# Rotary embedding on one core: the last add writes fp32 into the tile of x, and the copy from bf16 to fp32 on ScalarE goes

## The chip, the cores and the metric

The kernel runs on one core of a Trainium2 chip. The metric is the device time of one execution in microseconds (us). All runs quoted here were with a granted clock of 1.00, unless the text says otherwise. In the profile's lines DVE is VectorE, ACT is ScalarE, POOL is GpSimd and SP is SyncE. A name such as L94 is line 94 of the kernel's file. "Load" is a transfer from HBM to the on-chip memory, "store" one back. Both use the same 16 DMA engines.

A profiled span is about 1.8 us shorter than the time of the same run. Where the text compares moments, it uses the span.

## The reference, cut to what matters

```python
def setup_inputs():
    batch, seq_len, num_heads, head_dim = (8, 2048, 16, 64)
    # x: (8, 2048, 16, 64) fp32; cos, sin: (2048, 32) fp32

def reference(x, cos, sin):
    x_pairs = x.reshape(batch, seq_len, num_heads, head_dim // 2, 2)
    x1, x2 = x_pairs[..., 0], x_pairs[..., 1]
    out1 = x1 * cos - x2 * sin
    out2 = x1 * sin + x2 * cos
    return np.stack([out1, out2], axis=-1).reshape(batch, seq_len, num_heads, head_dim)
```

Input and output are 67.1 MB each, and each byte is moved once. Little is computed for each byte.

## The kernel before

The work is cut into 16 tiles of 128 partitions x 8 rows x 1024 values (4.19 MB), which are kept in five buffers (NX = 5). A tile is worked on in two pieces of four rows (128x4096). The first and the last tile are cut finer, into 4 pieces each, so there are 36 pieces: 30 of 128x4096, 2 of 128x2048 and 4 of 128x1024. Each piece passes through these steps:

```python
    def halve(j):                      # ScalarE: fp32 -> bf16
        i, k0, k1 = pieces[j]
        halved[j] = hpool.tile([P, 4, HD], bf16, name="xh", bufs=3)
        nc.scalar.copy(out=halved[j][:, : k1 - k0], in_=tiles[i][:, k0:k1])

    def rotate(j):                     # VectorE: three bf16 operations
        # ... (views of the tables and of the piece)
        nc.vector.tensor_tensor(out=rows(qt), in0=rows(xh), in1=tab(s_tab), op=mult)
        nc.vector.tensor_tensor(out=rows(xh), in0=rows(xh), in1=tab(c_tab), op=mult)
        # q_swap reads qt with the two members of each pair exchanged
        nc.vector.tensor_tensor(out=xh3, in0=xh3, in1=q_swap, op=add)
        rotated[j] = xh

    def widen(j):                      # ScalarE: bf16 -> fp32, then the store from ScalarE's queue
        i, k0, k1 = pieces[j]
        nc.scalar.copy(out=tiles[i][:, k0:k1], in_=rotated.pop(j)[:, : k1 - k0])
        # ... for each run of rows that is complete:
        nc.scalar.dma_start(out=out_t[b, g, :, r0:r1], in_=tiles[i][:, r0:r1])
        if k1 == K and i + NX < n:
            load(i + NX)               # SyncE's queue; waits until the store has freed the buffer

    # ... loads of tile 0, cos, sin, tiles 1 to 4; tables s_tab and c_tab made in bf16
        halve(0)
        for j in range(len(pieces)):
            if j + 1 < len(pieces):
                halve(j + 1)
            rotate(j)
            widen(j)
```

## Time and profile before

| | before |
|---|---|
| time, median of 4 runs | 318.59 us (318.53 to 318.70) |
| profiled span | 316.9 us |
| VectorE busy | 223.2 us (70%) |
| ScalarE busy | 230.0 us (73%) |
| moved | 134.76 MB, 425 GB/s over the span |

The first lines are from the page of the kernel before. They give the busy time of each engine, the span in 40 equal slices (one digit is the busy share of a slice in tenths, 9 meaning 90% or more), then the share of the 16 DMA engines' span that each queue's packets took.

```profile
DVE 223.2 (70%) x111; ACT 230.0 (73%) x73; POOL 0.2 (0%) x4
...
DVE  0189999999999596693967939588440999999112
ACT  4078899999998692976949679495803999997322
...
DMA  7999999999999999999999999999999999999997
...
q1 hardware_dynamic: 3712, 67.63, 50.1%
q10 hardware_dynamic: 2736, 67.11, 49.1%
```

The DMA row is 9 in every slice but the first and the last, while both compute engines have slices well below 9, many of 3 to 7. And the two queues together take 50.1% + 49.1% = 99.2% of all 16 DMA engines' time. There is hardly any time in which a DMA engine does nothing.

The groups by shape (count, busy us, mean ns of one, idle time of the engine before them and what ended it) give the cost of each step of a piece:

```profile
L75 ACT CAST xh<-xt 128x4096 bf16<-128x4096 f32 x30 | 108.1, 3603 | 50.7 <-DMA xt<-in_x_dram 45.4 <-ACT xt L105 5.4
L105 ACT CAST xt<-xh 128x4096 f32<-128x4096 bf16 x30 | 108.1, 3602 | 2.1 <-DVE xh L100 1.8
L94 DVE TENSOR_TENSOR qt<-xh,s_tab 128x4096 bf16<-128x4096 bf16 x30 | 68.8, 2292 | 56.6 <-ACT xh L75 55.8
L100 DVE TENSOR_TENSOR xh<-xh,qt 128x4096 bf16<-128x4096 bf16 x30 | 68.8, 2292 | 1.0
```

The view of waits (total us, times, longest) says why the compute engines idle. VectorE waits for ScalarE, and ScalarE waits for loads:

```profile
DVE qt L94 <- ACT xh L75: 70.3, 26, 12.9
ACT xh L75 <- DMA xt<-in_x_dram: 61.6, 13, 12.7
```

The chain that ended last is mostly DMA:

```profile
DMA 62%; ACT 26%; DVE 4%; issue 3%; another core or an unknown queue 2%; SPq 1%; ACTq 1%
```

The trace's records of issue and landing show the rate. Stores 0 to 10 land at 59.7, 79.1, 98.4, 118.6 us and so on, on average 19.44 us apart, although the first stores are issued every 14.7 us (35.94, 50.66, 65.35, 80.03). In the steady part a tile takes the DMA about 19.36 us (8.39 MB in and out, 433 GB/s).

### The profile page before, as it was taken

The page shows a single profiled execution, that of the slowest core. Times are in us where ns is not written, and L with a number is a line of the kernel's source. Part 1 is how long each engine was busy: PE and PEld are TensorE (multiplying, and loading weights), DVE is VectorE, ACT ScalarE, POOL GpSimd, SP SyncE. Part 2 cuts the span into 40 slices and gives each one's busy share as a digit, 9 for nine tenths or more (in the row PEclk, how much of TensorE's full clock was granted, in tenths as well). Part 3 has the DMA queues.
Part 4 walks back from the last instruction along what each step waited for, and adds up shares of the span by engine and source line. Part 5 has one row for each costly group of instructions (what it writes and reads, how often), then busy time and mean ns, then how long its engine had stood idle before and what let it go on. Part 6 is the DMA issues. An engine that isn't in the chain of part 4 may idle for free.

```text
span 316.9 us, 352 instructions
## 1 busy us (share of the span) xinstructions
DVE 223.2 (70%) x111; ACT 230.0 (73%) x73; POOL 0.2 (0%) x4
## 2 busy tenths in 40 slices
DVE  0189999999999596693967939588440999999112
ACT  4078899999998692976949679495803999997322
POOL 0000000000000000000000000000000000000000
DMA  7999999999999999999999999999999999999997
GB/s 304 424 463 405 455 397 401 459 438 422 455 405 463 397 460 401 459 414 448 443 418 455 405 459 405 455 405 459 418 443 447 414 428 430 424 433 439 442 414 302
DMA packets 6451, 134.76 MB, mean 425 GB/s; under 512 B 689, under 2 KB 1201, under 8 KB 1969
## 3 DMA queue, kind: packets, MB, share of 16 engines
q1 hardware_dynamic: 3712, 67.63, 50.1%
q10 hardware_dynamic: 2736, 67.11, 49.1%
q14 instruction: 3, 0.02, 0.0%
HBM read 67.63 MB, written 67.11 MB: 425 GB/s over the span
## 4 chain that ended last, share of the span: by engine, by line
DMA 62%; ACT 26%; DVE 4%; issue 3%; another core or an unknown queue 2%; SPq 1%; ACTq 1%
DMA xt<-in_x_dram 31%; DMA out_dram<-xt 28%; ACT xt L105 14%; ACT xh L75 12%; DMA sin_sb<-in_sin_dram 4%; DVE xh L100 1%; DVE xh L95 1%; DVE qt L94 1%; SPq L70 1%; ACTq L109 1%; DVE s_tab L121 0%; SPq L115 0%; DVE s_tab L122 0%; ACTq L105 0%
## 5 line engine op out<-in xcount | busy, mean ns | idle before, releaser
L75 ACT CAST xh<-xt 128x4096 bf16<-128x4096 f32 (+2 forms) x36 | 116.1, 3224 | 66.9 <-DMA xt<-in_x_dram 61.6
L105 ACT CAST xt<-xh 128x4096 f32<-128x4096 bf16 (+2 forms) x36 | 116.0, 3223 | 14.8 <-DVE xh L100 14.4
L94 DVE TENSOR_TENSOR qt<-xh,s_tab 128x4096 bf16<-128x4096 bf16 (+2 forms) x36 | 74.0, 2055 | 71.2 <-ACT xh L75 70.3
L100 DVE TENSOR_TENSOR xh<-xh,qt 128x4096 bf16<-128x4096 bf16 (+2 forms) x36 | 74.0, 2055 | 1.2
L95 DVE TENSOR_TENSOR xh<-xh,c_tab 128x4096 bf16<-128x4096 bf16 (+2 forms) x36 | 74.0, 2055 | 1.2
L121 DVE CAST s_tab<-sin_sb 128x512 bf16<-128x512 f32 x1 | 0.5, 453 | 14.4 <-DMA sin_sb<-in_sin_dram 14.4
L75 ACT ACT_TABLE_LOAD x1 | 1.3, 1283 | 0.7 <-PEq L147 0.7
L123 DVE CAST c_tab<-cos_sb 128x1024 bf16<-128x1024 f32 x1 | 0.7, 684 | 0.0
L122 DVE TENSOR_SCALAR s_tab<-sin_sb 128x512 bf16<-128x512 f32 x1 | 0.4, 442 | 0.0
L147 POOL MEMSET const-bfloat16-1.0<- 128x1 bf16 x1 | 0.1, 101 | 0.0
L147 POOL MEMSET const-uint8-127<- 128x1 uint8 x1 | 0.1, 101 | 0.0
L147 POOL MEMSET const-float32-0.0<- 128x1 f32 x1 | 0.1, 98 | 0.2 <-issue 0.2
L147 POOL MEMSET const-float32-1.0<- 128x1 f32 x1 | 0.1, 98 | 0.0
## 6 DMA issues: line engine op xcount, KB each, us to landing
out_dram<-xt ACTq DMA_DIRECT2D x15, 4096.0 KB, 38.6
xt<-in_x_dram SPq DMA_DIRECT2D x14, 4096.0 KB, 26.6
xt<-in_x_dram SPq DMA_DIRECT2D x2, 2048.0 KB, 16.3
xt<-in_x_dram SPq DMA_DIRECT2D x4, 512.0 KB, 24.1
xt<-in_x_dram SPq DMA_DIRECT2D x2, 1024.0 KB, 19.9
out_dram<-xt ACTq DMA_DIRECT2D x1, 2048.0 KB, 17.6
out_dram<-xt ACTq DMA_DIRECT2D x1, 1024.0 KB, 11.7
out_dram<-xt ACTq DMA_DIRECT2D x2, 512.0 KB, 4.1
```

Source lines behind the costliest of these rows:

```text
L70: nc.sync.dma_start(out=tiles[i][:, k0:k1], in_=x_t[b, g, :, k0:k1])
L75: nc.scalar.copy(out=halved[j][:, : k1 - k0], in_=tiles[i][:, k0:k1])
L94: nc.vector.tensor_tensor(out=rows(qt), in0=rows(xh), in1=tab(s_tab), op=mult)
L95: nc.vector.tensor_tensor(out=rows(xh), in0=rows(xh), in1=tab(c_tab), op=mult)
L100: nc.vector.tensor_tensor(out=xh3, in0=xh3, in1=q_swap, op=add)
L105: nc.scalar.copy(out=tiles[i][:, k0:k1], in_=rotated.pop(j)[:, : k1 - k0])
L109: nc.scalar.dma_start(out=out_t[b, g, :, r0:r1], in_=tiles[i][:, r0:r1])
L121: nc.vector.tensor_copy(out=s2[:, :, 0], in_=sin_flat)
L122: nc.vector.tensor_scalar_mul(s2[:, :, 1], sin_flat, -1.0)
L123: nc.vector.tensor_copy(out=c_tab.rearrange("p g k (i j) -> p (g k i) j", j=2), in_=cos_sb.rearrange("p g c -> p (g c)").to_broadcast([P, ...
L147: nc = _bacc.Bacc("TRN2", target_bir_lowering=False, num_devices=1)
```

## The change

The intent is to relieve ScalarE. VectorE's add writes its fp32 result directly over x in its tile, so that the second ScalarE copy (116.0 us busy in all) is not needed.

```diff
-        nc.vector.tensor_tensor(out=xh3, in0=xh3, in1=q_swap, op=add)
-        rotated[j] = xh
 
-    def widen(j):
+        y3 = tiles[i][:, k0:k1].rearrange("p k (a j) -> p (k a) j", j=2)
+        nc.vector.tensor_tensor(out=y3, in0=xh3, in1=q_swap, op=add)
+
+    def finish_piece(j):
         i, k0, k1 = pieces[j]
-        nc.scalar.copy(out=tiles[i][:, k0:k1], in_=rotated.pop(j)[:, : k1 - k0])
         g, b = groups[i]
 ...
             rotate(j)
-            widen(j)
+            finish_piece(j)
```

More of the change, by code (lines that the diff above doesn't have):

```diff
@@ L63 @@
         pieces += [(i, k0, k1) for k0, k1 in runs]
-    tiles, halved, rotated = {}, {}, {}
+    tiles, halved = {}, {}
     def load(i):
```

## The prediction

> **What bounds the kernel now.** The page's first two parts say DMA: the DMA row is 9 in all of the 40 slices but the first and last, at 425 GB/s over the 316.9 us span, while VectorE is busy 223.2 us (70%) and ScalarE 230.0 us (73%). The chain that ended last is 62% DMA. In the trace's issue and landing records, stores 0 to 10 land 19.3 to 20.2 us apart although ScalarE could prepare a tile every 14.7 us (stores issued at 35.94, 50.66, 65.35, 80.03); each load is issued when a store has freed its buffer. So a tile (4.19 MB in, 4.19 MB out) costs 19.36 us of DMA, 433 GB/s, and compute waits for it: the wait view has ScalarE waiting 61.6 us for loads and VectorE 70.3 us for ScalarE.
>
> **What the change does.** It removes 36 ScalarE copies (116.0 us busy), mostly off the bounding resource. It adds no instruction, but VectorE's final add now writes fp32. Today all three 4096-element VectorE operations take 2.292 us. The Trainium skill, "VectorE: DVE Perf Modes", section "The perf-mode tier table", gives a two-tensor operation double rate in bf16 only; its errata section gives (N+151)/0.96 ns for the fp32 add. The trace agrees with the same fixed term at double rate: (2048+151)/0.96 = 2291. So I expect the add at 4.42 us for 4096 elements, 2.29 for 2048, 1.22 for 1024. Bytes moved do not change.
>
> **The sum.** A full piece on VectorE goes from about 6.98 to 9.12 us with gaps, a tile from 14.0 to 18.24 us. All pieces: 30 x 9.12 + 2 x 4.84 + 4 x 2.71 = 294 us. VectorE busy becomes about 292 us (92%), ScalarE 114 us. VectorE starts rotating at 15.71 us as now (after the sin load), so unstarved it ends at about 310 us.
>
> **What is on the critical path.** 18.24 us per tile is below DMA's 19.36 by only 1.1 us. Store 0 is issued at about 35.1 us, and store i at about 35.1 + 18.24 i, always before store i-1 lands (about 39.5 + 19.36 i). So the store queue never runs dry, loads land almost when they do now, and each before VectorE needs it: tile 6 at about 105 us against 123, tile 14 at 260 against 269. VectorE runs nearly without a break, its backlog shrinking until the last pieces. The last row's load lands at about 308 us as now; VectorE is done with everything before at about 307. Then: halve 1.05, three operations 2.7, store 3.6. The removed last widening (1.04 us) is offset by 0.53 us of slower add. I expect under 1 us of change: the removed ScalarE work was hidden under DMA.
>
> **Predicted:** 318.0 us, 8 in 10 within 316.0 to 320.5. Faster by over 2%: 0.02; within 2%: 0.91; slower by over 2%: 0.07.
>
> **What the profile would show.** Add 4424 ns in the groups by form; VectorE 92%, ScalarE 36%; DMA row still 9s, about 426 GB/s; VectorE's waits for ScalarE fall from 70 us to under 10.
>
> **What would make it wrong.** Slack at the end is only 1 to 2 us, so an add above 4.5 us, or VectorE waiting for ScalarE (whose queue also holds the stores: store 11 now waits until 242.1 us for a load that shares its semaphore), would make it VectorE-bound at 320 to 325 us. If the mixed-type add kept double rate, DMA would still set the time, about 317.5 us.

## The result, and the profile after

| | before | after |
|---|---|---|
| time, median of 4 runs each | 318.59 us | 318.88 us (318.65 to 318.89) |
| ratio, 95% interval | | 1.0007 (0.9990 to 1.0024): the same |
| VectorE busy | 223.2 us (70%) | 291.4 us (92%) |
| ScalarE busy | 230.0 us (73%) | 116.3 us (37%) |
| one add of 128x4096 | 2.292 us | 4.425 us |

Ratios here and below are the mean time of one kernel's fast runs over that of the other's fast runs of the same rounds, so not quite the ratio of the medians quoted.

The same lines of the page, for the changed kernel:

```profile
DVE 291.4 (92%) x111; ACT 116.3 (37%) x37; POOL 0.2 (0%) x4
...
DVE  0199999999999999999999999999999999999993
ACT  4244441707044170805326080532608044350220
...
DMA  8999999999999999999999999999999999999997
...
q1 hardware_dynamic: 3712, 67.63, 50.1%
q10 hardware_dynamic: 2736, 67.11, 49.1%
```

ScalarE's busy time has halved and VectorE's row is now 9 in all slices but the first two and the last. The DMA row (but for its first slice) and the 99.2% have not moved, and neither has the time.

The groups by shape show the cost of the add, and the waits show that VectorE no longer waits for ScalarE at all. The roles have turned round: ScalarE waits 181.6 us for VectorE.

```profile
L102 DVE TENSOR_TENSOR xt<-xh,qt 128x4096 f32<-128x4096 bf16 x30 | 132.7, 4425 | 1.0
L75 ACT CAST xh<-xt 128x4096 bf16<-128x4096 f32 x30 | 107.1, 3604 | 164.5 <-DVE xt L102 159.2 <-DMA xt<-in_x_dram 5.2
L94 DVE TENSOR_TENSOR qt<-xh,s_tab 128x4096 bf16<-128x4096 bf16 x30 | 68.8, 2292 | 3.1
...
L102 DVE TENSOR_TENSOR xt<-xh,qt 128x1024 f32<-128x1024 bf16 x4 | 4.9, 1224 | 0.1
L102 DVE TENSOR_TENSOR xt<-xh,qt 128x2048 f32<-128x2048 bf16 x2 | 4.6, 2291 | 0.1
```

```profile
ACT xh L75 <- DVE xt L102: 181.6, 18, 11.3
DVE s_tab L121 <- DMA sin_sb<-in_sin_dram: 15.0, 1, 15.0
ACT xh L75 <- DMA xt<-in_x_dram: 9.7, 6, 2.8
```

The chain that ended last is now VectorE:

```profile
DVE 92%; DMA 4%; issue 2%; SPq 1%; DVEq 0%
```

This is a trap for a reader of profiles. The chain names VectorE for 92% of the span, yet the DMA engines are as full as they were. Two resources are at their limit at once, and a chain can follow only one of them. Which of them sets the time cannot be read from this page. The experiments decide it.

The timeline (start, duration, engine, line, operation) of one piece of the changed kernel gives VectorE's pitch: from 100.17 to 109.35 us is 9.18 us for a piece, so 18.36 us for a tile, against 19.36 us for the DMA.

```profile
100.17 2.29 DVE L94 TENSOR_TENSOR qt<-xh,s_tab 128x4096 bf16<-128x4096 bf16 x1
102.50 2.29 DVE L95 TENSOR_TENSOR xh<-xh,c_tab 128x4096 bf16<-128x4096 bf16 x1
104.82 4.43 DVE L102 TENSOR_TENSOR xt<-xh,qt 128x4096 f32<-128x4096 bf16 x1
109.28 0.34 ACTq L109 DMA_DIRECT2D out_dram<-xt  x1
109.35 2.29 DVE L94 TENSOR_TENSOR qt<-xh,s_tab 128x4096 bf16<-128x4096 bf16 x1
```

### The profile page after: what moved, and what is told of

It is laid out like the page before. It is cut to its first block, busy times and chain, and to the rows that moved or that the text cites. A ratio compares the mean times of both kernels' runs of the same rounds, so it can differ in the third digit from the quotient of the medians.

```text
span 317.1 us, 345 instructions
## 1 busy us (share of the span) xinstructions
DVE 291.4 (92%) x111; ACT 116.3 (37%) x37; POOL 0.2 (0%) x4
## 4 chain that ended last, share of the span: by engine, by line
DVE 92%; DMA 4%; issue 2%; SPq 1%; DVEq 0%
DVE xt L102 45%; DVE qt L94 23%; DVE xh L95 23%; DMA sin_sb<-in_sin_dram 4%; SPq L70 1%; DVEq L94 0%; DVE s_tab L121 0%; SPq L115 0%; DVE s_tab L122 0%; DVE c_tab L123 0%
## 5 line engine op out<-in xcount | busy, mean ns | idle before, releaser
L75 ACT CAST xh<-xt 128x4096 bf16<-128x4096 f32 (+2 forms) x36 | 115.1, 3224 | 191.4 <-DVE xt L102 181.6
L102 DVE TENSOR_TENSOR xt<-xh,qt 128x4096 f32<-128x4096 bf16 (+2 forms) x36 | 142.2, 3951 | 1.2
```

The lines of the kernel that those rows point to most:

```text
L102: nc.vector.tensor_tensor(out=y3, in0=xh3, in1=q_swap, op=add)
```

## The experiments

The theory T is that the transfers set the time of both kernels, and that VectorE's slower add just fits beside them. The rival R1 is that the change had two real effects that cancel, a gain from ScalarE and a loss from the add. The rival R2 is that VectorE alone sets the time of the changed kernel, as its chain says. Twelve kernels were run. "Wrong result on purpose" means that the arithmetic was cut for the sake of the measurement.

| run | result | median us | kernel before, same chip | ratio (95% interval) |
|---|---|---|---|---|
| dma_only | wrong | 318.16 | 318.80 | 0.9989 (0.9972 to 1.0005) |
| short_widen | wrong | 323.58 | 318.80 | 1.0132 (1.0096 to 1.0169) |
| half_widen | wrong | 318.90 | 318.67 | 1.0007 (0.9992 to 1.0022) |
| fp32_add_keep_copy | right | 324.65 | 318.80 | 1.0177 (1.0163 to 1.0190) |
| mixed | right | 318.73 | 318.80 | 0.9998 (0.9986 to 1.0010) |
| before_plus | right | 318.84 | 318.60 | 1.0006 (0.9993 to 1.0019) |
| after_plus | right | 318.79 | 318.60 | 1.0003 (0.9991 to 1.0015) |
| mixed_plus | right | 318.76 | 318.60 | 1.0005 (0.9993 to 1.0017) |
| after_plus_wide | right | 332.67 | 318.67 | 1.0434 (1.0416 to 1.0452) |
| after_tables_first | right | 320.60 | 318.60 | 1.0062 (1.0037 to 1.0087) |
| before_half_loads | wrong | 265.19 | 318.68 | 0.8321 (0.8308 to 0.8333) |
| after_half_loads | wrong | 317.22 | 318.68 | 0.9953 (0.9937 to 0.9970) |

### The transfers alone

```diff
-        halve(0)
         for j in range(len(pieces)):
-            if j + 1 < len(pieces):
-                halve(j + 1)
-            rotate(j)
             finish_piece(j)
```

> All loads and stores stay, all halving, rotating and widening goes (wrong result on purpose). Theory T (the 134.76 MB at about 433 GB/s set the time of both kernels): 316 to 318.5 us, at most 0.7% under the kernel before. Rival R1 (the change had two real effects that cancel: less ScalarE work gains, a slower add loses): the time falls well below both, under 310 us, since both are gone. Rival R2 (the changed kernel is set by VectorE alone and the transfers have room): also under 310 us.

Measured: 318.16 us. From its page:

```profile
DVE 1.4 (0%) x3; POOL 0.2 (0%) x4
...
DMA  8999999999999999999999999999999999999997
```

With no work on the pieces at all, the kernel takes what both kernels take, to within 0.3%. T holds and R1's gain has no room to exist: with these transfers in these queues, less than 1 us can be won from the kernel before by removing compute.

### VectorE alone, and ScalarE alone: half of the loads taken away

```diff
-        for k0, k1 in load_runs(i):
+        for k0, k1 in (load_runs(i) if i in (0, n - 1) else [(0, 4)]):
...
-        nc.scalar.copy(out=halved[j][:, : k1 - k0], in_=tiles[i][:, k0:k1])
+        r0 = k0 if i in (0, n - 1) else 0
+        nc.scalar.copy(out=halved[j][:, : k1 - k0], in_=tiles[i][:, r0 : r0 + k1 - k0])
```

The same edit was made to both kernels.

> The kernel before, but of tiles 1 to 14 only rows 0 to 3 are loaded and both pieces are halved from them (wrong result on purpose): 29.4 MB less to load, compute as it was. T: the transfers no longer set the time; ScalarE does, at 14.7 us a tile: about 258 to 268 us, faster by 16 to 19%.

> The changed kernel with the same 29.4 MB less to load. Its VectorE work has no gaps today, so T says that it takes over as the limit at once: 317 to 319 us, at most 0.6% faster, with the DMA row well below 9. If the transfers alone had set the time, it would fall as the kernel before does.

Measured: 265.19 us and 317.22 us. First the page of the kernel before with half loads (engines' busy time, ScalarE's row, DMA's row):

```profile
DVE 223.2 (85%) x111; ACT 230.1 (87%) x73; POOL 0.2 (0%) x4
...
ACT  4029799999999999999999999999999999999760
...
DMA  7999959797999999999999999999999999996997
```

Then the page of the changed kernel with half loads (engines' busy time, VectorE's row, DMA's row):

```profile
DVE 291.4 (92%) x111; ACT 115.9 (37%) x37; POOL 0.2 (0%) x4
...
DVE  0199999999999999999999999999999999999995
...
DMA  7999678978787895978879697877969966290996
```

Relieved of 29.4 MB, the kernel before falls to the next limit, ScalarE, which is then at 9 from the sixth slice to the fourth from the end, and issues a store every 14.66 us. Its DMA row is still 9 nearly everywhere (a tile's 6.29 MB at 433 GB/s would take 14.5 us, by calculation), so here too two limits lie close together, and compute by itself may need a little less than 265 us. The changed kernel falls by 0.5% only, with a DMA row that has slices of 5 and 6 and even 0: VectorE's work by itself takes 317.2 us. So the changed kernel has two limits within 1 us of each other, 318.2 us for the transfers and 317.2 us for VectorE. Before the change the compute engines had at least 53 us of room under the DMA limit (318.7 - 265.2); the change has used nearly all of it.

### Each half of the change alone

The first half: the bf16 add stays, and the ScalarE copy is cut to 16, then to 512, of every 1024 columns.

```diff
-        nc.scalar.copy(out=tiles[i][:, k0:k1], in_=rotated.pop(j)[:, : k1 - k0])
+        nc.scalar.copy(
+            out=tiles[i][:, k0:k1, :16], in_=rotated.pop(j)[:, : k1 - k0, :16]
+        )
```

> The kernel before with its bf16 add, but the ScalarE copy writes only 16 of every 1024 columns (wrong result on purpose), so the ScalarE work goes alone, without the slower add. T: 317 to 319 us, no gain above 0.5%, ScalarE busy falls to about 125 us. R1: faster by over 1%, since the gain is no longer paid back by the add.

> The kernel before with a ScalarE copy of 512 of every 1024 columns (wrong result on purpose): half of the ScalarE work that the change removes, with the bf16 add. T: removing it gains nothing: 317.5 to 319.5 us. If less ScalarE work itself makes the transfers slower, as the run with 16 columns could be read, about 320 to 322 us, with load packets that take longer than 1213 ns in each tile. R1: about half of a gain, under 316 us.

Measured: 323.58 us with 16 columns (six runs, 321.12 to 324.84) and 318.90 us with 512. In neither case is there a gain, so R1's gain is not seen. With 512 columns T's range holds. With 16 columns T's range was missed on the other side: less ScalarE work made the kernel 1.3% slower. The trace's packet records tell how, though not why. A packet of 32 KB takes 1213 ns on its DMA engine nearly always, and 16 engines x 32768 bytes / 1213 ns = 432 GB/s is the rate that all these kernels reach. In the run with 16 columns 370 such packets took over 1230 ns, in the kernel before 39, and in the run with 512 columns 43. The excess over 1213 ns, summed over the packets and divided by 16, is 3.8 us against 0.8 and 0.9. It comes in short bursts, one per tile, mostly in load packets. The rest of the loss (the span is 4.7 us longer than that of the kernel before) is at the end: in the last 10 us the DMA engines are idle for 3.6 us against 1.9. In this run each load lands some 4 us before the next store lands, and in the steady part of the other profiled runs at full load it leads by 5 us or more. That the two streams disturb each other at such a distance is a guess. It was not tested, and the cause stays open. Long packets are not peculiar to a shorter ScalarE copy: the next run, with all the copies, has 145 of them (2.8 us of excess over all packets), most of that before 85 us.

The other half: the fp32 add of the changed kernel, with a ScalarE copy of each piece put back, in place.

```diff
     def finish_piece(j):
         i, k0, k1 = pieces[j]
+        nc.scalar.copy(out=tiles[i][:, k0:k1], in_=tiles[i][:, k0:k1])
```

> The changed kernel with a ScalarE copy of each piece put back, in place on the fp32 tile (right result): the slower add alone, ScalarE about 230 us busy again. T: 319 to 321 us; the add of 4.42 us fits, and only the last one-row copy (about 1.0 us) is added at the end. R1: slower by over 1.5% (over 323 us), since the loss is no longer offset.

Measured: 324.65 us, 1.8% slower. T's range of 319 to 321 us was missed, and R1's number ("over 323") was met. The trace of the profiled run (323.67 us, span 321.9) says where it went. Its timeline near the twelfth store reads:

```profile
242.18 4.43 DVE L102 TENSOR_TENSOR xt<-xh,qt 128x4096 f32<-128x4096 bf16 x1
246.32 0.34 ACTq L110 DMA_DIRECT2D out_dram<-xt  x1
246.71 3.60 ACT L75 CAST xh<-xt 128x4096 bf16<-128x4096 f32 x1 [5.59 <-DMA xt<-in_x_dram]
...
250.34 2.29 DVE L94 TENSOR_TENSOR qt<-xh,s_tab 128x4096 bf16<-128x4096 bf16 x1 [3.74 <-ACT xh L75]
```

The store at 246.32 us, store 11, was issued when load 13 landed (246.25 us, by the landing records), since the two share a semaphore (number 103 in the records). The next halving stood behind that store in ScalarE's queue, and VectorE waited 3.74 us for it. The kernel before has the same wait (its store 11 was held until 242.13 us) and does not feel it in its total, because its VectorE has room. At the end VectorE waits another 0.21 + 0.58 us between small pieces that ScalarE now has to copy, and the last copy adds 1.04 us. Together that is 5.6 us. VectorE also began 0.5 us earlier than in the changed kernel, which leaves 5.1; the span is 4.8 us longer. So the loss is not the add's length as such (4.43 us here too). It is that with this add VectorE can no longer make up for a wait. The run after_plus (below) has the same hold without the copies: there too store 11 shares semaphore 103 with load 13 and was issued only when that had landed (243.11 after 243.03 us), yet VectorE's pitch grew only once, from 9.19 to 9.53 us, where it grows from 9.18 to 12.82 us here. It follows that taking the ScalarE copies away is of use after all to the slower add: it keeps VectorE nearly free of waits. Each half of the change, taken alone to nearly its full extent, was slower; together they are even.

### How much VectorE work there is room for

In "mixed" every fourth piece keeps the bf16 add and the ScalarE copy:

```diff
+        if j % 4 == 1:
             nc.vector.tensor_tensor(out=xh3, in0=xh3, in1=q_swap, op=add)
             rotated[j] = xh
+        else:
+            y3 = tiles[i][:, k0:k1].rearrange("p k (a j) -> p (k a) j", j=2)
+            nc.vector.tensor_tensor(out=y3, in0=xh3, in1=q_swap, op=add)
...
+        if j in rotated:
             nc.scalar.copy(out=tiles[i][:, k0:k1], in_=rotated.pop(j)[:, : k1 - k0])
```

> Every fourth piece (9 of 36) keeps the bf16 add and the ScalarE copy, the others add in fp32 (right result). VectorE has 7 x 2.13 + 0.53 + 1.07 = 16.5 us less to do than in the changed kernel. T: 317.5 to 319 us, VectorE busy about 275 us with idle time of its own. R2 (VectorE alone sets the changed kernel's time, as 92% of its chain says): about 302 us.

Measured: 318.73 us. From its page:

```profile
DVE 274.9 (87%) x111; ACT 144.5 (46%) x46; POOL 0.2 (0%) x4
...
DVE  0199999999999999999999999999580799999981
```

VectorE has 16.5 us less to do than in the changed kernel and idles in the slices of 5 and 0 (where store 11 is held until load 13 lands, 243.06 us), and the time is the same. R2 (302 us) falls.

The opposite direction: one more VectorE multiplication per piece in three kernels.

```diff
+        nc.vector.tensor_tensor(out=extra, in0=xh[:, 0, :256], in1=xh[:, 0, :256], op=mult)
         nc.vector.tensor_tensor(out=rows(qt), in0=rows(xh), in1=tab(s_tab), op=mult)
```

> The kernel before with one more VectorE multiplication of 128x256 bf16 in each of the 36 pieces; (128+151)/0.96 = 291 ns and about 0.03 us of gap each, 11.6 us in all. T: unchanged, 318.2 to 319.5 us: VectorE (70% busy) has room.

> The changed kernel with the same extra multiplication. T says that VectorE's room is used up, so all of it shows: VectorE ends its work at about 312.5 + 11.6 = 324 us, the time is 329 to 331.5 us. If VectorE had room of more than 1 or 2 us left, the time would be under 328 us; if DMA alone still set the time, it would stay at 319.

> The mixed kernel (every fourth piece with bf16 add and ScalarE copy) with the same extra multiplication. It has 16.5 us less VectorE work than the changed kernel, so 11.6 us more should be swallowed: 317.5 to 319.5 us. If the margin isn't room in VectorE's time but something else, it is above 322 us.

Measured: 318.84, 318.79 and 318.76 us. The second is far from the 329 to 331.5 us expected. The dose was the error, as the timeline of that run shows:

```profile
288.73 4.42 DVE L104 TENSOR_TENSOR xt<-xh,qt 128x4096 f32<-128x4096 bf16 x1
293.07 0.28 DVE L95 TENSOR_TENSOR extra<-xh 128x256 bf16<-128x256 bf16 x1
...
293.27 2.29 DVE L96 TENSOR_TENSOR qt<-xh,s_tab 128x4096 bf16<-128x4096 bf16 x1
```

The extra operation lasts 0.28 us by itself, but it starts 0.08 us before the add has ended and lies in the gap that was there anyway. The pitch of a piece rose from 9.18 to 9.19 us. So these three runs show only that nothing was taken away from VectorE, and they test nothing. The operation was then made four times as wide, with its cost worked out from this pitch:

```diff
+        nc.vector.tensor_tensor(out=extra, in0=xh[:, 0], in1=xh[:, 0], op=mult)
         nc.vector.tensor_tensor(out=rows(qt), in0=rows(xh), in1=tab(s_tab), op=mult)
```

> The changed kernel with one more VectorE multiplication in each of the 36 pieces, now 128x1024 bf16. The 128x256 one of the run before turned out to cost only 0.01 us of VectorE's time per piece (9.19 against 9.18 us), as it ran in the gap and the tail of its neighbour; 768 more elements at two per cycle add (768/2)/0.96 = 0.40 us each, so some 0.41 us per piece and 14.8 us in all. T (VectorE has no room left beside the transfers): 331 to 334 us. If the transfers alone set the time and VectorE had 10 us of room or more: under 324 us.

Measured: 332.67 us, against 318.88 for the changed kernel. From its page:

```profile
DVE 310.0 (94%) x147; ACT 116.0 (35%) x37; POOL 0.2 (0%) x4
...
DVE  0199999999999999999999999999999999999995
...
DMA  8999999999999999999999999999999999880985
```

The 0.41 us per piece (14.8 us in all) show almost in full, 13.8 us, and the DMA row begins to show holes near the end. The traces show where the missing 1 us is: VectorE's last operation ends 15.1 us later (327.56 against 312.50 us), but the last store then lands 2.6 us after it instead of 3.6. So the changed kernel has next to no room left on VectorE. That a tile takes VectorE 1.0 us less than the DMA (18.36 against 19.36 us; 19.18 with the added work, still less) is no room, because VectorE starts only at 16.26 us: 16.26 + 296.24 us of work + 3.63 us to the last landing make 316.1 of the 317.1 us span. Its time no longer waits for ScalarE, and it would grow with any VectorE work that is added.

### An earlier start of VectorE

```diff
-        load(0)
-        nc.sync.dma_start(out=cos_sb, in_=cos_t)
         nc.sync.dma_start(out=sin_sb, in_=sin_t)
+        nc.sync.dma_start(out=cos_sb, in_=cos_t)
+        load(0)
```

> The changed kernel with the sin and cos loads issued before those of x, so that VectorE begins some 8 to 10 us earlier (at about 6 us instead of 15). T: the transfers set the time, 317.5 to 319 us; VectorE then waits for loads later. R2 (VectorE alone sets it): about 309 us.

Measured: 320.60 us (six runs, 319.39 to 322.36). R2's 309 us falls again: VectorE began with the tables 11.4 us earlier (3.6 instead of 15.0 us) and then waited 12.9 us for ScalarE, which waited 166.3 us for loads. T's range was missed by 1.6 us. The profiled run was the fastest (319.39 us) and shows a first slice of 244 GB/s against 298, so the transfers start slower. What the slower of the six runs lost was not profiled and stays open.

## Why the prediction was right

The time, 318.88 us, lies inside the range, and the change is within noise as forecast. Point by point:

- **The transfers bound the kernel.** Right for the kernel before: the transfers alone take 318.16 us. The changed kernel has a second limit at the same place, VectorE, which runs without a wait from 16.26 to 312.50 us.
- **The add at 4.42 us for 4096 elements, 2.29 for 2048, 1.22 for 1024.** Right: 4.425, 2.291 and 1.224 us. The section "The perf-mode tier table" of the Trainium skill's page "VectorE: DVE Perf Modes", which gives the double rate for bf16 and not for fp32, was the reason to expect it, together with the formula of its errata section, and the trace agrees.
- **A piece of 9.12 us.** It measured 9.18. The gap from the add to the next multiplication is 0.10 us (104.82 + 4.43 to 109.35 in the timeline), and I had taken 0.03 as between the multiplications. Over all pieces VectorE needed 296.2 us instead of 294. It also started 0.55 us later, as the sin load landed at 14.96 us. It ended at 312.5 us instead of 310.
- **Loads land before they are needed.** Right: tile 6 at 107.2 us (forecast 105), tile 14 at 262.1 (forecast 260).
- **The store queue never runs dry.** Right, but barely. Store 14 was issued at 292.88 us, 2.1 us before store 13 landed at 294.99.
- **The last row's load lands at about 308 us and sets the end.** Wrong. It landed at 296.7 us. The packet records fit the reading that the stores came later and left the DMA to the loads: from 292 to 297 us packets of 0.88 MB of loads began, against 0.32 MB in the kernel before. VectorE set the end instead. That the total came out right all the same is partly luck: the forecast path (308 + 1.05 + 2.7 + 3.6 = 315.4 us) and the real one (312.5 + 3.6 = 316.1 us) end 0.7 us apart.
- **VectorE's waits for ScalarE under 10 us; VectorE 92%, ScalarE 36%.** Right: no such wait is listed, and 92% and 37%.
- **"The removed ScalarE work was hidden under DMA."** Right for the transfers alone and with half of the copies. With nearly all copies gone and the bf16 add kept, the kernel was 1.3% slower, mostly by longer packets of unknown cause, which the prediction had no place for.
- **What would make it wrong: VectorE waiting for ScalarE because of store 11.** In the changed kernel it did not happen: store 11 was issued at 237.80 us, before load 13 landed at 242.75. That was luck, since in the trace's records the two no longer share a semaphore there (101 and 103), which the prediction did not foresee. It saved little: in after_plus, where they share it, VectorE's pitch grew by 0.34 us, once. With the copies put back they share it again, the wait happened, and the kernel took 324.65 us, within the 320 to 325 that the prediction gave for that case.

The direction of the small difference was not forecast rightly (318.0 expected, 318.88 measured). The step that was mis-sized is VectorE's total, by 2.2 us, and its start, by 0.55 us.

## What to carry to other kernels

When the DMA row is full, time the transfers alone before touching compute: here that one run shows that less compute could not win 1 us. A change that leaves the time as it is can still use up the room: with 29.4 MB less to load, the kernel before became 53 us faster, the changed one less than 2. When two resources are full at once, the chain names only one of them, so take work away from each in turn. And measure an added cost by the pitch of the loop rather than by the operation's own duration.

## What the Trainium skill lacked or had wrong

- "VectorE: DVE Perf Modes": no page gives a time for a two-tensor operation with two bf16 inputs and an fp32 output. Here that add took 4425 ns for 4096 elements, against 2292 ns with a bf16 output. The errata section states (N+151)/0.96 ns for the fp32 add at 512 and 2048 elements; it gives 4424 ns here and fits the mixed form at 4096 elements too.
- The same page, section "The DRAIN you can't avoid", speaks of a next operation that cannot issue until the pipe is empty, and only a clause at the end of its first paragraph says that one that is not held starts earlier. Here an independent 128x256 multiplication started 0.08 us before the end of the add in front of it, and added 0.01 us to a piece though it lasts 0.28 us. The section gives no size for this.
- "DMA: Bandwidth & Descriptors", section "Where 436 GB/s comes from", says that for transfers between HBM and SBUF the HBM side, about 358 GB/s, binds. The sentence does not say that it is meant for two cores at work; the same page's note on its measurements does. With one core at work, loads and stores together ran at 433 GB/s here, near the section's fabric figure of 435.
- "Perfetto Trace Analysis", section "Identifying the Most-Contended Engine", advises HBM utilization instead of occupancy for DMA. Here the two said the same of both kernels (99.2% of the 16 engines' span, 425 GB/s), and neither was enough to name the limit: with half of the loads taken from the kernel before, the DMA row is 9 nearly throughout at 400 GB/s, and ScalarE sets the time.
- No page that I read has the time of one packet as such: 32 KB took 1213 ns on one engine, loads and stores alike, in both kernels. Nor does one say when load packets take longer, as in the run with 16 columns (370 packets over 1230 ns).
